# Two model blocks on one core: modulation sums on VectorE in the second block, grouped column sums, split spreads, and a last head-block in smaller chunks

## The chip, the cores and the metric

The kernel runs on one core of a Trainium2 chip. The metric is the device time of one execution in microseconds; lower is better. The program has no loop on the device: it is unrolled into 17908 instructions on the engines TensorE (PE, with its weight loads PEld), VectorE (DVE), ScalarE (ACT), GpSimd (POOL) and SyncE (SP, whose queue issues the weight loads).

## What is computed

For 256 tokens of width 1024, a first block of two layers (attention, recurrence and convolution, mixed and projected) is followed by a second block with a modulated norm, two mixers and an expert step. What the change touches belongs to the second block:

```python
def second_block(x, c, ctx, c_ctx, w_ada, b_ada, ...):
    s_c, s_cc = jax.nn.silu(c), jax.nn.silu(c_ctx)
    mod_lat = (s_c @ w_ada[l] + b_ada[l])[:, None, :]        # six parts of 1024: 0 to 5
    mod_ctx = s_cc @ w_ada[l] + b_ada[l]
    sh1, sc1, gt1, sh2, sc2, gt2 = jnp.split(mod_lat, 6, axis=-1)
    h_lat = rmsnorm(x, g_norm1) * (1.0 + sc1) + sh1          # parts 1 and 0, also for ctx
    ...                                                      # MLA attention and mLSTM on h_lat, h_ctx
    x = x + gt1 * (concat([mla_lat, ml_lat]) @ w_out)        # part 2
    h2 = rmsnorm(x, g_norm2) * (1.0 + sc2) + sh2             # parts 4 and 3
    return x + gt2 * peer(h2, w_pq, sub_keys, u, v)          # part 5

q = rmsnorm(q, g_qn); k = rmsnorm(k, g_kn)                   # per head over 128 + 64 values, in the MLA
```

In `peer` each token takes 16 experts for each of 8 heads; an expert is a row of 1024 values of `u` and 1024 of `v`. The row is gathered, its dot product with h2 goes through Gelu and a gate, and the result weighs the row of `v`.

## The kernel before

Activations are held transposed, 128 features on the partitions and 256 tokens in the free dimension, as 8 such tiles. Most projections are exact to fp32 by a split: ScalarE rounds a raw weight tile `w` (128x1024, 512 KB) into `wh` (L323), VectorE takes the rest `wl` (L268), and TensorE runs three fp32r matmuls for each pair (`wsplit`, `mm3`). Raw tiles come through `wload` (L314) on SP's queue into a ring of `NRAW` = 5 buffers with the tag `w`; the split pair has three buffers.

The order on each engine is made when the kernel is built. `at(us)` gives the following instructions a priority in planned time, `wload` puts a load 25 us ahead of its user, and a planner issues what is ready in that order, with its own model of durations and waits. On the chip each engine runs its list in order, so an instruction that waits holds everything behind it on that engine.

The six modulation parts are products of one vector with 1024x1024 matrices `wada`, eight tiles of 512 KB each:

- Parts 1, 0, 2, 4 and 3 run on TensorE in `part` (L963): eight loads through a ring of two buffers with the tag `wm`, 32 matmuls with 32 columns of weights, grouped four by four beside each other in the array, a copy (L966), two transposes. They are called by `hook`: the first three within layer 0, the last two within layer 1, at the planned times `mt`. With `np` = 5 the generator `modparts` has nothing to do.
- Part 5, the gate of the experts' result, runs during the expert step: `gate_sums` loads its tiles into the ring `w` and sums them on VectorE with `modsum` into `gs`, row by row times the scalar `sc0`, as a side task between the experts' dot products.

In the second block (`second`) the order of the program is: norms, `kvr`, `keys`, queries, `values` for both token sets (`proj` and `natural` use the ring `w`), the scans of the mLSTM gates, then the MLA heads. There `wkv` and two `wuq` tiles are loaded into the ring too and are used without a split until the heads and the value product `vml` are done. The sum of squares of each head's keys and queries is built with one-column matmuls, `ssk` and `ssq`, the squares as weights and a column of ones as the moving operand. The reciprocal roots go back to rows by spreads: 16 times VectorE scales the identity (`dg`, two buffers) and TensorE multiplies it by ones. Then come `mla` (scores, softmax, product) and `cells` (mLSTM, with a broadcast of the running maximum `Mr` by an fp32 matmul of 8 rows, 512 columns), interleaved by the string `PATTERN`, and `project` with weights `wo2`.

In `peer`, `experts` issues for each of 256 pairs of head-block and pick one gather on POOL (L1559) of 128 rows of 8 KB into one of nine buffers `G`, a dot product on VectorE (L1562), and after a chunk of picks the Gelu (L1566), the product with the gate, and for each pick a diagonal (L1575) and two fp32 matmuls of 512 columns. Chunks have four picks; in the last of 16 head-blocks they are 4, 4, 4, 2, 1, 1.

Of the kernel before, what the change touches and what calls it, by code (L numbers as in the profile page):

```python
# [8 lines left out]
F32 = mybir.dt.float32  # L9
F32R = mybir.dt.float32r  # L10
# [9 lines left out]
T = 256  # L20
# [105 lines left out]
def pack(inp):  # L126
# [97 lines left out]
    o["bgate"] = f["b_ada_2"][:, 5120:]  # L224
# [8 lines left out]
P = dict(np=5, glu=14, kv=35, kk=40, q=41, cmp=46, cmpd=5, w1n=62, cv0=32, cvd=35, att=57, attd=5, mix=137, woa=131, ln=145, pw2=160, wob=138, mod=5, ll=25000, sl=6000, nm=3, mt=(62, 80, 170, 243, 270), sp=29, L0=10, L1=196, S=369, B=500, cx=125, h1=2, h2=6, X=16, lri=37, lnk=7, tp=2, tq=0, ta=0, ml=40, mld=2.6, rt=36, g0=-32, ga=104, gb=161, gc=157)  # L233
# [7 lines left out]
def program(tc, A, dbg=lambda *a: None, stop=99):  # L241
# [66 lines left out]
    NRAW, NSP, NWA, NWM = 5, 3, 2, 2  # L308
# [175 lines left out]
    SLOTS = dict(g1=2048, g2=2048, g3=2048, g4=2048, g5=2048, g6=2048, gz4=1024, cz=1024, lu=2180, cs=512, silc=258,  # L484
# [459 lines left out]
    def modulation():  # L944
# [13 lines left out]
        def part(m):  # L958
# [18 lines left out]
            if m == 4:  # L977
                mg["pr"] = mk(cp, [128, 8], tag="mgpr")
                stt(mg["pr"], modt[:, 32:40, 0], 1.0, P2("g2"), add, mul)

        return [prep] + [lambda m=m: part(m) for m in (1, 0, 2, 4, 3)[:int(P["np"])]]

    def modsum(acc, m, k):

        w = wload(A["wada"][m, k], [128, 4, 256]).rearrange("p j c -> p (j c)")
        s = sc0[:, k:k + 1]
        if k == 0 and m != 5:
            ts(acc, w, s, None, mul)
        else:
            stt(acc, w, s, acc, mul, add)  # L990

    def modparts():
        for m in (4, 3)[int(P["np"]) - 3:]:
            acc = mk(b1, [128, 1024], tag="wm", bufs=NWM)
            for k in range(8):
                modsum(acc, m, k)
                if k == 7:
                    tp = psum("c", [128, 8])
                    for d in range(8):
                        mm(tp[:, d:d + 1], acc[:, d * 128:d * 128 + 128], ones[:, 0:1], True, True)  # L1000
                    o = modt[:, m * 8:m * 8 + 8, 0]
                    tt(o, tp, P2("bada")[:, m * 8:m * 8 + 8], add)
                    if m == 4:
                        mg["pr"] = mk(cp, [128, 8], tag="mgpr")
                        stt(mg["pr"], o, 1.0, P2("g2"), add, mul)
                if k % 2:
                    yield

    def second(C0, S):
# [187 lines left out]
        for d in range(2):  # L1197
            for b in range(2):
                tr(mnp[:, d, b], Mr[d][:, 256 + b * 128:384 + b * 128], ident[0:8, 0:8])
        emn = mk(b1, [128, 2, 2, 4], tag="emn")  # L1200
# [14 lines left out]
        values(0, X + 11)  # L1215
        keys(1, X + 15)

# [7 lines left out]
        ssk = psum("t", [128, 4, 4])  # L1225
        ckf = ckv.rearrange("p w t -> p (w t)")
        skf = skr.rearrange("p w t -> p (w t)")
        for h in range(4):
            acc = psum("acc", [128, 512])
            mm(acc, wkv[:, h * 128:(h + 1) * 128], ckf, True, True)  # L1230
            sq = slot(("blk", "cw2")[h % 2], 512)
            act.activation(sq, acc, AF.Square)
# [17 lines left out]
        ssq = psum("o", [128, 2, 4])  # L1250
        for h in range(0, 4, 2):
# [7 lines left out]
            for q in range(2):  # L1259
                for b in range(2):  # L1260
                    bs = slice(b * 128, b * 128 + 128)
                    mm(ssq[:, b, h + q:h + q + 1], sq[:, q, bs], ones[:, 0:1], True, False)
                    mm(ssq[:, b, h + q:h + q + 1], sqr[:, h // 2, bs], C(f"sel{q}"), False, True)
        values(1, X + 20)
        for q in range(4):
# [11 lines left out]

        v = mk(b1, [128, 24], tag="ssv")
        ts(v[:, 0:16], ssk.rearrange("p h q -> p (h q)"), 1.0 / 192, EPS, mul, add)
        ts(v[:, 16:24], ssq.rearrange("p b h -> p (b h)"), 1.0 / 192, EPS, mul, add)  # L1280
# [5 lines left out]
        krf = krr.rearrange("p w t -> p (w t)")  # L1286
        for h in range(4):
# [5 lines left out]
            tt(kn[:, h], kn[:, h], bc, mul)  # L1293
            hs = (lo64, hi64)[h % 2]
# [375 lines left out]
```

## Time and profile before

| what | value |
|---|---|
| median of 3 runs | 1406.02 us (1400.61 to 1406.84) |
| profiled execution | 1406.54 us, span 1404.6 us |
| TensorE busy | 1214.2 us, 86% |
| VectorE busy | 995.6 us, 71% |
| ScalarE busy | 528.6 us, 38% |
| GpSimd busy | 291.9 us, 21% |
| granted TensorE clock, mean | 0.938 |
| DMA | 387.50 MB, 276 GB/s over the span |

The busy time counts from an instruction's start to its modelled end; matmuls overlap, so a busy TensorE need not be at its peak. The granted clock is given as a share of 2.4 GHz. "DMA share" is the mean busy share of the core's 16 DMA engines. In a row, `c<-wm,silc` is the tile that is written and those that are read; a bracket at the end of a row tells how long the engine idled before it and what ended that. The chain of waits is the sequence of work that ended last, followed back from the last instruction.

### The profile page before, as it was taken

The page shows a single profiled execution, that of the slowest core. Times are in us where ns is not written, and L with a number is a line of the kernel's source. Part 1 is how long each engine was busy: PE and PEld are TensorE (multiplying, and loading weights), DVE is VectorE, ACT ScalarE, POOL GpSimd, SP SyncE. Part 2 cuts the span into 40 slices and gives each one's busy share as a digit, 9 for nine tenths or more (in the row PEclk, how much of TensorE's full clock was granted, in tenths as well). Part 3 has the DMA queues.
Part 4 walks back from the last instruction along what each step waited for, and adds up shares of the span by engine and source line. Part 5 has one row for each costly group of instructions (what it writes and reads, how often), then busy time and mean ns, then how long its engine had stood idle before and what let it go on. Part 6 is the DMA issues. An engine that isn't in the chain of part 4 may idle for free.

```text
span 1404.6 us, 17908 instructions
## 1 busy us (share of the span) xinstructions
PE 1214.2 (86%) x6050; PEld 798.9 (57%) x6050; DVE 995.6 (71%) x2454; ACT 528.6 (38%) x1130; POOL 291.9 (21%) x279
## 2 busy tenths in 40 slices
PE   6999899899979999999898978688868786877787
PEld 5987669698848888856795433243323332323333
DVE  6898865599987674455768766777676767667554
ACT  5635544344754544345453222222222222112211
POOL 0000000000000000000022444334444443443442
PEclk9999999899999987999999998999898999899989
DMA  8677446557403532410459999998999999999996
GB/s 323 193 282 263 168 162 218 169 170 245 133 21 108 165 98 75 132 33 1 151 193 423 421 422 421 421 407 349 421 422 412 422 421 413 414 422 421 417 409 273
DMA packets 71339, 387.50 MB, mean 276 GB/s; under 512 B 8401, under 2 KB 9425, under 8 KB 38226
## 3 DMA queue, kind: packets, MB, share of 16 engines
q0 software_dynamic: 36864, 268.45, 46.4%
q1 hardware_dynamic: 34386, 117.93, 24.8%
q8 instruction: 48, 0.79, 0.2%
q14 instruction: 41, 0.34, 0.1%
HBM read 385.30 MB, written 1.05 MB: 275 GB/s over the span
## 4 chain that ended last, share of the span: by engine, by line
PE 49%; DMA 27%; DVE 8%; issue 8%; POOL 5%; ACT 2%; POOLq 0%; DVEq 0%; SPq 0%; ACTq 0%
DMA G<-uv,eix 24%; PE acc L256 22%; PE acx L256 11%; PE s L256 6%; POOL G L1559 5%; DVE G L1562 4%; PE t L256 3%; PE o L256 2%; DMA wm<-wada 2%; PE c L963 2%; PE s L412 1%; DMA w<-wpq 1%; PE t L259 1%; PE c L256 1%; PE o L645 1%
## 5 line engine op out<-in xcount | busy, mean ns | idle before, releaser
L1562 DVE SCALAR_TENSOR_TENSOR G<-G,hn 128x1024 f32<-128x1024 f32 x256 | 313.5, 1225 | 176.9 <-DMA G<-uv,eix 173.5
L1559 POOL DMA_INDIRECT G<-uv,eix x256 | 284.4, 1111 | 443.0 <-PE o L256 134.4
L323 ACT ACTIVATE wh<-w 128x1024 fp32r<-128x1024 f32 (+2 forms) x142 | 148.5, 1048 | 192.2 <-PE acc L256 120.3
L268 DVE TENSOR_TENSOR wl<-w,wh 128x1024 fp32r<-128x1024 f32 (+2 forms) x142 | 171.5, 1210 | 62.6 <-ACT wh L323 61.3
L256 PE MATMUL t<-G,dg 128*128 128x512 f32 x256 | 146.7, 657 | 69.6 <-ACT dg L1575 69.6
L256 PE MATMUL c<-G,dg 128*128 128x512 f32 x256 | 147.2, 659 | 61.7 <-ACT dg L1575 61.7
L256 PE MATMUL acc<-hh,wh 128*128 128x256 f32 x608 | 178.5, 297 | 11.4 <-ACT wh L323 4.3
L256 PE MATMUL acc<-hh,wl 128*128 128x256 f32 x608 | 178.0, 295 | 2.0 <-DVE wl L268 2.0
L256 PE MATMUL acc<-hl,wh 128*128 128x256 f32 x608 | 166.5, 287 | 1.6 <-DVE hl L268 1.6
L1575 ACT ACTIVATE dg<-cst,w 128x128 f32<-128x128 f32 x256 | 89.4, 394 | 144.9 <-PE o L256 61.6
L256 PE MATMUL o<-G,dg 128*128 128x512 f32 x256 | 141.9, 638 | 0.0
L256 PE MATMUL acx<-G,dg 128*128 128x512 f32 x256 | 141.5, 636 | 0.0
L1566 ACT ACTIVATE s<-s 128x4 f32<-128x4 f32 (+1 forms) x66 | 13.5, 205 | 331.8 <-DVE G L1562 331.7
L256 PEld LDWEIGHTS t<-G,dg 128*128 128x128 f32 x256 | 50.2, 207 | 147.8 <-ACT dg L1575 95.3
L256 PEld LDWEIGHTS acc<-hh,wh 128*128 128x128 f32 x608 | 120.0, 198 | 19.5 <-ACT wh L323 5.1
L256 PEld LDWEIGHTS c<-G,dg 128*128 128x128 f32 x256 | 50.3, 207 | 133.7 <-ACT dg L1575 82.6
L256 PEld LDWEIGHTS acc<-hh,wl 128*128 128x128 f32 x608 | 120.4, 198 | 7.1 <-issue 2.8
L256 PEld LDWEIGHTS acc<-hl,wh 128*128 128x128 f32 x608 | 113.9, 193 | 5.3 <-issue 2.4
L262 DVE SCALAR_TENSOR_TENSOR g<-lu,pb,g 128x256 f32<-128x256 f32 x264 | 115.2, 480 | 0.2
L256 PEld LDWEIGHTS o<-G,dg 128*128 128x128 f32 x256 | 53.0, 207 | 69.5 <-issue 69.5
L256 PEld LDWEIGHTS acx<-G,dg 128*128 128x128 f32 x256 | 52.9, 206 | 68.9 <-issue 68.9
L1054 POOL MEMSET lu<- 128x16 f32 x1 | 0.4, 444 | 401.0 <-DVE g L262 401.0
(494 smaller groups left out, 2000.1 us busy)
## 6 DMA issues: line engine op xcount, KB each, us to landing
w<-w SPq DMA_DIRECT2D x64, 512.0 KB, 4.5
wm<-wada SPq DMA_DIRECT2D x40, 512.0 KB, 5.1
wa<-cw SPq DMA_DIRECT2D x16, 512.0 KB, 5.0
w<-woa SPq DMA_DIRECT2D x16, 512.0 KB, 3.5
w<-wpq SPq DMA_DIRECT2D x16, 512.0 KB, 3.5
w<-w2t SPq DMA_DIRECT2D x12, 512.0 KB, 3.5
w<-wob SPq DMA_DIRECT2D x8, 512.0 KB, 6.2
w<-w2v SPq DMA_DIRECT2D x8, 512.0 KB, 3.9
```

The lines of the kernel that those rows point to most:

```text
L256: pe.matmul(out, lhsT, rhs, start=start, stop=stop)
L259: pe.transpose(out, in_, ident)
L262: (e or dve).scalar_tensor_tensor(out, a, s, b, op0=op0, op1=op1)
L268: return (e or dve).tensor_tensor(out, a, b, op=op)
L323: act.activation(hi, w, AF.Copy)
L412: pe.matmul(acc[j:j + 32], ones[:, 0:32], sq[:, q] if square else srcs[i + q], start=i + q < 4, stop=i + q >= n - 4, tile_position=(0, j))
L645: pe.matmul(hps[32 * j:32 * j + 32], blk[:, q4 * 4 + j], w[:, j], start=q4 == 0, stop=q4 == 3, tile_position=(0, 32 * j))
L963: pe.matmul(acc[32 * j:32 * j + 32], sc[:, k], w[:, j], start=k == 0, stop=k == 7, tile_position=(0, 32 * j))
L1559: pool.indirect_dma_start(out=G, out_offset=None, in_=A["uv"], in_offset=bass.IndirectOffsetOnAxis(ap=eix[b][:, h, k:k + 1], axis=0))
L1562: dot = dve.scalar_tensor_tensor(G[:, 0:D], G[:, 0:D], 1.0, hn[b], op0=mul, op1=mul, accum_out=s[:, j:j + 1])
L1566: act.activation(s[:, 0:n], s[:, 0:n], AF.Gelu)
L1575: act.activation(dg, ident, AF.Copy, scale=w[:, j:j + 1])
```

## The change

Parts 2, 4 and 3 no longer run in the layers, and part 5 no longer in the expert step: `sums` computes all four on VectorE in the second block, in the order 4, 3, 2, 5. Each call of `more` loads one tile into the ring `w` and adds it; the calls stand after the projections, in the loops over heads, and after each step of `PATTERN`. Each part ends with four grouped matmuls, a copy and two transposes. The ring of raw tiles has four buffers instead of five, and the accumulator `ms` takes the room. The sums of squares of keys and queries become matmuls with 32 columns of ones, four heads beside each other in the array; their result goes back to columns by a matmul with `bd4`. The spread of the keys' roots is done with transposes, a split into two fp32r parts, and a broadcast from four rows; the broadcast of `Mr` in `cells` is split in the same way. Part 5 is turned into rows by `gate_rows` in the expert step. The last head-block has the chunks 4, 4, 2, 2, 1, 1, 1, 1.

```diff
-    NRAW, NSP, NWA, NWM = 5, 3, 2, 2
+    NRAW, NSP, NWA, NWM = 4, 3, 2, 2
...
-        return [prep] + [lambda m=m: part(m) for m in (1, 0, 2, 4, 3)[:int(P["np"])]]
...
+        return [prep] + [lambda m=m: part(m) for m in (1, 0)]
+
+    def sums(m):
+
+        acc = slot("ms", 1024)
+        for k in range(8):
+            w = wload(A["wada"][m, k], [128, 4, 256]).rearrange("p j c -> p (j c)")
+            if k == 0:
+                ts(acc, w, sc0[:, k:k + 1], None, mul)
+            else:
+                stt(acc, w, sc0[:, k:k + 1], acc, mul, add)
+            yield
+        tot = psum("c", [128, 256])
+        for j in range(4):
+            pe.matmul(tot[32 * j:32 * j + 32], ones[:, 0:32], acc[:, j * 256:j * 256 + 256], start=True, stop=True,
+                      tile_position=(0, 32 * j))
+        rows = mk(b1, [128, T], tag="tmp", bufs=3)
+        act.activation(rows, tot, AF.Copy)
+        tp = psum("c", [128, 2, 128])
+        for q in range(2):
+            tr(tp[:, q], rows[:, q * 128:q * 128 + 128], ident)
...
+        rest = [sums(m) for m in (4, 3, 2, 5)]
+
+        def more():
+
+            while rest and next(rest[0], 0) == 0:
+                rest.pop(0)
...
         kvr(0, S + 5)
+        more()
         keys(0, S + 9)
+        more()
...
+        id8 = slot("sc", 8, F32R)[0:8]
+        act.activation(id8, ident[0:8, 0:8], AF.Copy)
...
+            act.activation(Mh[d], Mr[d][:, 256:512], AF.Copy)
+            tt(Ml[d], Mr[d][:, 256:512], Mh[d].bitcast(F32), sub)
...
         for h in range(4):
+            more()
             acc = psum("acc", [128, 512])
             mm(acc, wkv[:, h * 128:(h + 1) * 128], ckf, True, True)
...
-            for q in range(4):
-                qs = slice(q * 128, q * 128 + 128)
-                mm(ssk[:, h, q:q + 1], sq[:, qs], ones[:, 0:1], True, False)
-                mm(ssk[:, h, q:q + 1], skf[0:64, qs], ones[0:64, 0:1], False, True)
+        mm(sumk, ones[0:64], skf[0:64], True, False)
+        for h in range(4):
+            pe.matmul(sumk[32 * h:32 * h + 32], ones[:, 0:32], sqk[:, h], start=False, stop=True, tile_position=(0, 32 * h))
...
+        for q in range(4):
+            mm(ss[:, q * 4:q * 4 + 4], rowk[:, q * 128:q * 128 + 128], C("bd4"), True, True)
...
         for h in range(4):
             bc = psum("s", [128, 512])
-            for q in range(4):
-                dg = mk(b1, [128, 128], tag="dg", bufs=2)
-                ts(dg, ident, rk[:, h * 4 + q:h * 4 + q + 1], None, mul)
-                mm(bc[:, q * 128:(q + 1) * 128], ones, dg, True, True)
+            one = id8[0:4, h:h + 1].broadcast_to([4, 128])
+            mm(bc, one, rkh, True, False)
+            mm(bc, one, rkl, False, True)
             tt(kn[:, h], kn[:, h], bc, mul)
+            more()
...
-                        mm(mb, ident[0:8, dh:dh + 1].broadcast_to([8, 128]), ml_[:, :, None, :].broadcast_to([8, 2, 2, 128]),
-                           True, False)
+                        for i, m in enumerate((Mh[d], Ml[d])):
+                            m = m.rearrange("p (t c) -> p t c", c=128)[:, :, None, :].broadcast_to([8, 2, 2, 128])
+                            mm(mb, id8[:, dh:dh + 1].broadcast_to([8, 128]), m, i == 0, False)
...
         for c in PATTERN:
             at(X + P["ml"] + P["mld"] * n)
             n += 1
             next(steps[c], None)
+            more()
...
-        def gate_sums():
-            for k in range(8):
-                modsum(gs, 5, k)
-                yield 1
+        def gate_rows():
             for hf in range(2):
                 gp = pst("g", [128, 512])
-                mm(gp, ones, gs[:, hf * 512:hf * 512 + 512], True, True)
+                for k in range(4):
+                    dg = mk(pp, [128, 128], tag="dg", bufs=3)
+                    ts(dg, ident, modt[:, 40 + hf * 4 + k, 0:1], None, mul)
+                    mm(gp[:, k * 128:k * 128 + 128], ones, dg, True, True)
+                    yield 1
...
-            experts(r % 8, r // 8, U0 + 16 * PICK * r, 4 if r == 0 else 2, (4, 4, 4, 4) if r < 15 else (4, 4, 4, 2, 1, 1))
+            experts(r % 8, r // 8, U0 + 16 * PICK * r, 4 if r == 0 else 2, (4, 4, 4, 4) if r < 15 else (4, 4, 2, 2, 1, 1, 1, 1))
```

## Rows read from the trace of the kernel before

**Rows 1.** Stages: PE, PEld, DVE, ACT, POOL busy us, PEclk, DMA share, GB/s

```profile
419.00:541.00 122.00, 115.13 (x789) 100.49 (x788) 87.86 (x218) 62.06 (x112) 3.03 (x8) 0.93 0.40 125
541.00:573.00 32.00, 31.80 (x142) 27.99 (x142) 8.06 (x20) 10.26 (x21) 0.00 (x0) 0.73 0.17 55
573.00:613.00 40.00, 37.44 (x145) 25.70 (x144) 23.82 (x51) 16.11 (x23) 0.00 (x0) 0.96 0.37 119
613.00:665.00 52.00, 51.09 (x237) 33.27 (x236) 28.77 (x102) 29.39 (x83) 0.96 (x1) 0.90 0.00 1
724.00:1391.00 667.00, 531.37 (x1322) 241.48 (x1321) 461.09 (x1149) 162.65 (x403) 284.05 (x256) 0.93 1.00 414
```

**Rows 2.** Parts: chain 155 to 270 (shares; start, us), waits on `wm`, VectorE's timeline

```profile
by line: PE acc L256 32.0%; DMA wm<-wada 20.0%; PE acx L256 13.7%; PE c L963 9.2%; PE s L256 5.7%; PE t L259 3.0%; PE o L811 2.0%; DVE g L749 2.0%; PE s L412 1.9%; DVE g L262 1.2%; issue 1.2%; ACT L745 1.1%; DVE wl L268 1.0%; DVE g L268 0.9
...
183.68 1.00 PE c L963 x16
...
  DMA wm<-wada: 23.8, 20
...
255.91 3.22 DVE L460 SCALAR_TENSOR_TENSOR g<-XT,pb,t 128x256 f32<-128x256 f32 x8 [4.24 <-PE t L256]
```

**Rows 3.** Timeline: convolution's sums copied, its projection begins; layer 0, then 1

```profile
182.56 0.38 ACT L415 ACTIVATE tmp<-s 128x256 f32<-128x256 f32 x1
201.96 0.60 PE L256 MATMUL acc<-g,wa 128*128 128x256 f32 x2
...
412.55 0.39 ACT L415 ACTIVATE tmp<-s 128x256 f32<-128x256 f32 x1
427.31 2.08 PE L256 MATMUL acx<-g,wa 128*128 128x256 f32 x4
```

**Rows 4.** Chain, heads (start, us, what, records); last row by stage

```profile
542.62 2.29 PE t L256 x16
545.96 3.30 PE t L256 x16
549.26 2.86 PE acx L256 x6
552.12 7.92 PE t L256 x32
561.19 4.77 PE acc L256 x16
569.11 3.47 PE o L256 x32
...
550.00:560.00 10.00, 10.00 (x38) 9.32 (x37) 0.00 (x0) 0.00 (x0) 0.00 (x0) 0.50 0.00 0
```

**Rows 5.** Chain: fp32r of 512 columns, broadcast with mask, fp32 of 512 columns

```profile
588.62 4.08 PE acx L256 x18
613.82 1.26 PE s L256 x3
624.51 1.72 PE s L256 x4
```

**Rows 6.** One line's operations: ns min/median/max, first and last start

```profile
L262 DVE SCALAR_TENSOR_TENSOR gs<-w,sc,gs x8: 1265/1280/1285, 895.8 to 954.0; 128x1024 f32<-128x1024 f32 x8
```

**Rows 7.** SP's queue in order of time; landing of `wada` tiles

```profile
508.76 0.33 SPq L314 DMA_DIRECT2D w<-wukv  x1
527.90 10.94 SPq L314 DMA_DIRECT2D w<-w2v  x4
...
DMA to landing us min/median/max: 3.2/5.2/9.6
```

**Rows 8.** Expert step: `wada` loads (ns, first and last), a dip, the end

```profile
L314 SPq DMA_DIRECT2D w<-wada x8: 328/328/328, 725.4 to 900.8; - x8
...
950.00:960.00 10.00, 7.16 (x17) 3.27 (x16) 7.37 (x20) 3.48 (x7) 2.61 (x3) 0.83 0.64 220
...
1385.58 1.13 PE L256 MATMUL t<-G,dg 128*128 128x512 f32 x2 [1.12 <-ACT dg L1575]
```

More of the change, by code (lines that the diff above doesn't have):

```diff
@@ L992, in modparts @@
-    def modparts():
-        for m in (4, 3)[int(P["np"]) - 3:]:
-            acc = mk(b1, [128, 1024], tag="wm", bufs=NWM)
-            for k in range(8):
[L996 to L1007, printed above, removed]
+        return [prep] + [lambda m=m: part(m) for m in (1, 0)]
@@ L1199, in second @@
                 tr(mnp[:, d, b], Mr[d][:, 256 + b * 128:384 + b * 128], ident[0:8, 0:8])
+        id8 = slot("sc", 8, F32R)[0:8]
+        act.activation(id8, ident[0:8, 0:8], AF.Copy)
+        Mh = [slot(n, T, F32R)[0:8] for n in ("rows", "ang")]
+        Ml = [slot(n, T, F32R)[0:8] for n in ("silc", "hidr")]
+        for d in range(2):
+            act.activation(Mh[d], Mr[d][:, 256:512], AF.Copy)
+            tt(Ml[d], Mr[d][:, 256:512], Mh[d].bitcast(F32), sub)
         emn = mk(b1, [128, 2, 2, 4], tag="emn")
@@ L1215, in second @@
         values(0, X + 11)
+        more()
         keys(1, X + 15)
+        more()
         accq = proj(1, (3, 4), X + 10)
@@ L1249, in second @@
             rope2(u[:, r], qr[:, r])
-        ssq = psum("o", [128, 2, 4])
+        sumq = psum("o", [128, T])
+        sqs = []
         for h in range(0, 4, 2):
@@ L1258, in second @@
             act.activation(qn[:, h:h + 2], acc, AF.Copy, scale=P2("gqn"))
[L1259 to L1263, printed above, removed]
+            sqs += [sq[:, 0], sq[:, 1]]
+        for h in range(4):
+            pe.matmul(sumq[32 * h:32 * h + 32], C(f"sel{h % 2}").broadcast_to([128, 32]), sqr[:, h // 2], start=True, stop=False,
+                      tile_position=(0, 32 * h))
+        for h in range(4):
+            pe.matmul(sumq[32 * h:32 * h + 32], ones[:, 0:32], sqs[h], start=False, stop=True, tile_position=(0, 32 * h))
+        rowq = slot("cw2", T)
+        act.activation(rowq, sumq, AF.Copy)
+        more()
         values(1, X + 20)
+        more()
         for q in range(4):
@@ L1276, in second @@
             so.append(th)
+        ss = psum("s", [128, 24])
+        for q in range(4):
+            mm(ss[:, q * 4:q * 4 + 4], rowk[:, q * 128:q * 128 + 128], C("bd4"), True, True)
+        for b in range(2):
+            mm(ss[:, 16 + b * 4:20 + b * 4], rowq[:, b * 128:b * 128 + 128], C("bd4"), True, True)
         v = mk(b1, [128, 24], tag="ssv")
-        ts(v[:, 0:16], ssk.rearrange("p h q -> p (h q)"), 1.0 / 192, EPS, mul, add)
-        ts(v[:, 16:24], ssq.rearrange("p b h -> p (b h)"), 1.0 / 192, EPS, mul, add)
+        ts(v, ss, 1.0 / (32 * 192), EPS, mul, add)
         rk = rsqrt(b1, v, [128, 24], "rk", 1)
@@ L1286, in second @@
         krf = krr.rearrange("p w t -> p (w t)")
+        rp = psum("s", [4, 512])
+        for q in range(4):
+            tr(rp[:, q * 128:q * 128 + 128], rk[:, q * 4:q * 4 + 4], ident)
+        rkh, rkl = slot("blk", 512, F32R)[0:4], slot("cw2", 512, F32R)[0:4]
+        act.activation(rkh, rp, AF.Copy)
+        tt(rkl, rp, rkh.bitcast(F32), sub)
         for h in range(4):
             bc = psum("s", [128, 512])
-            for q in range(4):
-                dg = mk(b1, [128, 128], tag="dg", bufs=2)
-                ts(dg, ident, rk[:, h * 4 + q:h * 4 + q + 1], None, mul)
-                mm(bc[:, q * 128:(q + 1) * 128], ones, dg, True, True)
+            one = id8[0:4, h:h + 1].broadcast_to([4, 128])
+            mm(bc, one, rkh, True, False)
+            mm(bc, one, rkl, False, True)
             tt(kn[:, h], kn[:, h], bc, mul)
+            more()
             hs = (lo64, hi64)[h % 2]
@@ L1420, in project @@
                 yield
-        steps = dict(m=mla(), c=cells(), a=project(0), x=modparts())
+        steps = dict(m=mla(), c=cells(), a=project(0))
         n = 0
@@ L1427, in second @@
             next(steps[c], None)
-        for c in "mcxa":
+            more()
+        while rest:
+            more()
+        for c in "mca":
             for _ in steps[c]:
@@ L1593, in peer @@
         gtb = mk(pp, [128, 2, 512], tag="gtb")
-        gs = mk(pp, [128, D], tag="gs")
-        at(B + 10)
-        pool.memset(gs, 0.0)
-        nc.sync.dma_start(gs[0:1], A["bgate"])
-        def gate_sums():
-            for k in range(8):
-                modsum(gs, 5, k)
-                yield 1
+        def gate_rows():
             for hf in range(2):
                 gp = pst("g", [128, 512])
-                mm(gp, ones, gs[:, hf * 512:hf * 512 + 512], True, True)
+                for k in range(4):
[3 more added lines that the diff above has]
+                    yield 1
                 act.activation(gtb[:, hf], gp, AF.Copy)
@@ L1621, in peer @@
             if r == 3:
-                side.append(gate_sums())
+                side.append(gate_rows())
             if r == 10:
@@ L1645, in hook @@
             return
-        for i in range(min(int(P["nm"]), len(steps)) if l == 0 else len(steps)):
-            at(P["mt"][int(P["np"]) - len(steps)])
+        for i in range(len(steps)):
+            at(P["mt"][2 - len(steps)])
             steps.pop(0)()
```

30 lines of the change are left out of this document (13 added, 17 removed).

## The prediction, written before the changed kernel had run

> **What bounds the kernel now.** I read the busy time of the engines by stage first, then the chain that ended last, then single waits. The stages [rows 1] show two kinds of kernel. From 724 to 1391 us the DMA share is 1.00 at 414 GB/s: the expert gathers run and the transfer sets the pace, while TensorE is busy 531 of 667 us and VectorE 461. Before that TensorE sets it: in the second block, 419 to 665 us, it is busy 115.1 of 122, 31.8 of 32, 37.4 of 40 and 51.1 of 52 us, while VectorE has 34, 24, 16 and 23 us idle, 97 together. The third thing to see is where TensorE is busy with little: from 550 to 560 it is busy 10.00 us at a granted clock of 0.50, the lower of its two levels, with VectorE and ScalarE at 0.00 [rows 4].
>
> The sum is made against the profiled execution's own 1406.54 us (span 1404.6 and 1.94 around it), 0.5 above the median of the three runs.
>
> **1. Three modulation parts leave the layers.** Before, parts 2, 4 and 3 run on TensorE in layer 0's attention and at the start of layer 1. Of the chain from 155 to 270 us, waits on their weights are 20.0% and their matmuls 9.2%, 33.6 of 115 us [rows 2]: the upper bound. What comes back is less, since something else is late next. In layer 1 VectorE has the norm's diagonals ready, but the spread's matmuls stand behind a part that waits for its load, and VectorE waits 4.24 us for them until 255.91 [rows 2]. Without that the four matmuls need some 1.2 us, start included: 2.9 to 3.0 saved, and with the two later bursts of the part, at 1.00 us each [rows 2], 4.9. In layer 0 I compare the same stretch in both layers, from the copy of the convolution's sums to its projection: 182.56 to 201.96 = 19.4 us with parts between, 412.55 to 427.31 = 14.8 without [rows 3]. Attention runs beside it on VectorE and ScalarE and doesn't get faster, so I take 4 of the 4.6. Layer term: **-9**, from -3 to -16.
>
> **2. Column-grouped sums.** Removed are 32 one-column matmuls for the keys, 2.29 + 3.30 + 7.92 = 13.5 us in the chain, and 16 for the queries, 3.47 [rows 4]: 17.0 on TensorE, all on the path, since VectorE idles beside them. Added: one full 512-column sum of the rope part at 0.86 us (1.72 for four records of that form [rows 5]); four grouped ones of 512 and eight of 256, by the grouped form's 16 records of 256 columns in 1.00 us [rows 2] about 1.0 each; six small ones on `bd4`, 12 records at 0.11 (3.47/32), 1.3. Together 4.2, net -12.8. The projections between them ran at the lower clock too: 22 records of 256 columns took 2.86 + 4.77 = 7.6 us [rows 4] where half of a 512-column record, 0.215, each would be 4.7, so 2.9 more if the clock now stays up: -15.7. ScalarE is next in line, and is busy 10.3 us in the whole stretch [rows 1], shorter than TensorE's new 15 or so. I take **-16**; if the clock stays down -10, at best -19.
>
> The Trainium skill, in TensorE: Matmul & The Clock Gate (Part 1), says that the clock follows the engine's activity and falls in idle gaps. Read by it, removing filler could also cool the array. The row of the stretch says that busy one-column work didn't keep it up, so by the row nothing is lost; by the rule a gap behind late weights costs, and that is the third rival below.
>
> **3. Split spreads.** The keys' spread loses 16 diagonals and 16 small fp32 matmuls for two copies, four transposes and eight fp32r matmuls of 512 columns at 0.23 (4.08/18 [rows 5]): the matmul time is equal within 1 us, but the stop and go on the two diagonal buffers goes; it is most of the 2.6 us that TensorE idles between 573 and 613 [rows 1]. In the cells, eight fp32 broadcasts, 1.26 each with the mask [rows 5], become two fp32r ones, 0.46 with 0.12 for the mask: 0.68 each, 5.4 in all. The scalars `id8`, `Mh`, `Ml` cost five short operations beside TensorE work. Neither form at K=4 or 8 in fp32r stands in the trace; bounds are 0.23 (the 128-row form) and 0.43 (a pass of fp32). At the upper bound the cells gain 2.3. Of the 8 together a third is hidden by VectorE and ScalarE, so **-5**, from 0 to -8.
>
> **4. What is added in the second block.** 32 sums of 128x1024 on VectorE, at 1.28 us [rows 6] 41 us, against 97 idle, and 32 loads of 512 KB through the ring of raw weights, which goes from five buffers to four. Their cover is VectorE's idle time, and it is uneven. Loads of this ring are issued in the order of the program. After `wkv` (508.76 [rows 7]) and the two `wuq`, which stay in their buffers until the heads are done, one buffer is left. Five sum tiles pass through it ahead of the values' weights: 5 x (5.2 landing [rows 7] + 1.3) = 32 us from about 516, so the values' weights, issued from 527.9 before [rows 7], go at about 549 and are split near 557, when TensorE, 16 us earlier now, would want them: 5 lost. Later 16 sums fall, by the pattern, beside the cells: 28.8 + 20.5 = 49.3 of 52 us of VectorE there. Behind each stand softmax maxima, reciprocals and scales, and TensorE waits for those; a third of the 16 lands on the path, 7. The four short ends (grouped sums, copy, two transposes) cost 1 together. A load that comes late stops VectorE as it stopped TensorE in the parts, 23.8 us in 20 waits [rows 2]. Bounds: 0 (all hidden) and 32 x (1.28 + 1.19) = 79. I take **+13**, nearer to the lower end, because VectorE's idle total is more than twice the sums. In the layers the fourth buffer costs nothing: a tile is used every 2.9 us, so four reach 11.5 us ahead and landing takes 5.2; its cover is that lead, and 1 us would go where a split waits.
>
> **5. The gathers.** Eight loads of part 5, 4.19 MB, leave the stage [rows 8]; at 421 GB/s they are 10.0 us of a queue that is never idle. The first came at 725, as the queue was filling, so 9. From 950 to 960 the share was 0.64 at 220 GB/s [rows 8]: TensorE stood behind a late score weight whose load had queued behind these eight on SP, and gathered rows weren't freed. That is 201 of 421 for 10 us, 4.8, and the dip's edges on both sides some 2.6 more; I take 6. The new `gate_rows` (eight diagonals, eight small matmuls, two copies) lies beside the transfers. **-15**, from -8 to -18.
>
> **6. The last head-block.** Before the last chunk of four, TensorE waits 1.12 us for its weights [rows 8] and is then busy to the end. Chunks of two start it earlier; two more Gelu calls and products at 0.2 us lie in the gaps. **-1.5**, from 0 to -2.
>
> **Sum.** -9 - 16 - 5 + 13 - 15 - 1.5 = -33.5: **1373 us**.
>
> **Rivals.** (a) *All sums hidden*: VectorE's idle time takes them and the loads arrive in time; step 4 costs 1 or 2, and with 3 more from the layers the time is 1373 - 12 - 3 = 1358. For it: 97 us idle. Against: the crowded cells. (b) *Starved second block*: the one free buffer holds the sums, then the values' and the output gate's weights back, TensorE waits and its clock falls to the lower level, at which the grouped sums and heads take twice as long: step 2 falls to -10, step 4 rises to +27, 1373 + 20 = 1393. For it: the weights' order [rows 7] and the clock of 0.50 [rows 4]. Against: TensorE has the values' product with `wkv` to do meanwhile. This is the case to which the skill's clock rule would lead. (c) *The sums become the path*, the slower end: every sum and a wait of 1.19 before it stops VectorE in a stretch where TensorE waits for it, 79 us in place of 13: 1373 + 66 = 1439. It decides from step 4 above 46.5, half of all sums and waits; the idle 97 us speak against it. (d) *The gathers don't get shorter*, because the issue on GpSimd or TensorE paces them: step 5 is 0, 1388. Against: a share of 1.00 over 667 us.
>
> **Chances.** Forecast (1364 to 1384) 0.45; (a) 0.20; (b) and (d) together 0.22; gains lost to within the bound 0.08; (c) 0.05. About 0.5%, 7 us, is what a measurement here can tell from no change. Slower by more than that 0.05, within 0.08, faster 0.87. The range leaves out less than 2 in 10: from 1352, all of (a) but its best, to 1394, the end of (b).
>
> **What would show it.** Step 1: no `wada` load under 260 us but those of parts 1 and 0, layer 1's first projection some 9 us earlier. Step 2: the heads' stretch, 31 us from first head to last query sum, takes about 15 at a clock near 1.0. Step 3: no diagonals in the key spread. Step 4: busy VectorE in the cells near 50 of their time and, if it costs, waits of VectorE on `w<-wada` and a longer cells stretch. Step 5: no `wada` load among the gathers, no dip, from first gather to last 15 us less. Wrong would be: second block not shorter than before, or the DMA share under 1 in the gathers.

## The result, and the profile after

The changed kernel takes 1385.77 us (median of 4 runs, 1383.0 to 1386.17) beside 1403.33 for the kernel before (4 runs, 1400.61 to 1406.84). The ratio is 0.9867, with a 95% interval of 0.9845 to 0.9889, so it is 18.7 us faster (15.6 to 21.8): the forecast side and inside the range of 1352 to 1394, but only 56% of the 33.5 us that the sum had. The profiled execution shortens from a span of 1404.6 to 1383.6 us.

The page of the changed kernel: TensorE has 24 us less to do than before, VectorE 24 more.

```profile
span 1383.6 us, 17499 instructions
PE 1190.4 (86%) x5826; PEld 778.7 (56%) x5826; DVE 1019.2 (74%) x2475; ACT 530.0 (38%) x1139; POOL 300.1 (22%) x278
```

Its stages, the lines that answer to [rows 1] (stretch, its length, then PE, PEld, DVE, ACT and POOL busy, granted clock, DMA share, GB/s): the heads from the first head's matmul to the last query sum, the values up to the last matmul that turns the sums of squares back into columns (`bd4`), the spreads up to the matmul behind the first softmax, the cells up to the output projection, and the gathers from the first issue to the last.

```profile
531.92:550.90 18.98, 18.11 (x82) 8.87 (x80) 10.88 (x20) 12.47 (x27) 1.80 (x1) 1.00 0.44 156
550.90:568.80 17.90, 17.00 (x71) 12.70 (x70) 11.34 (x17) 9.89 (x14) 0.00 (x0) 0.90 0.68 220
568.80:600.57 31.77, 27.03 (x100) 15.03 (x99) 27.81 (x46) 8.07 (x16) 0.00 (x0) 0.89 0.72 245
600.57:651.96 51.39, 47.86 (x248) 33.17 (x249) 39.16 (x112) 32.44 (x87) 0.00 (x0) 0.97 0.36 123
710.70:1361.30 650.60, 525.80 (x1322) 239.43 (x1321) 448.50 (x1140) 160.57 (x399) 292.15 (x256) 0.92 1.00 413
```

The heads run at full clock now, where [rows 4] had 0.50. The next thing to see is the third line: VectorE is busy for 27.8 of 31.8 us there and TensorE has 4.7 us idle. The chain of that stretch (568.8 to 601 us, shares by engine and line) says why:

```profile
by line: DVE ms L261 34.4%; DMA w<-wada 30.1%; DVE g L267 14.2%; issue 6.8%; PE acx L255 3.0%; DVE onat L261 2.8%; ACT blk L1348 2.7%; PE s L255 2.5%; DVE mmx L1343 2.4%; DVE cw L267 1.1%; DVE mmx L261 0.5%; DVE modt L267 0.5%; DVEq L261 0.
```

The sums and the loads that they wait for are two thirds of it. The waits on loads of the ring in the second block that come to 2 us or more (what waited, for what, us, times, longest); those of VectorE are for the sums' tiles alone:

```profile
DVE ms L261 <- DMA w<-wada: 14.6, 10, 2.9
ACT wh L322 <- DMA w<-w2o: 4.6, 2, 2.8
DVE ms L264 <- DMA w<-wada: 2.3, 2, 1.6
```

To see where each kernel wins and loses, I divide the profiled executions at five marks: the load of the context tokens (the end of layer 1's attention), the first head's matmul, the first softmax maximum on VectorE, the first gather, and the last dot product of a gathered row. Times in us, with the ratio to the kernel before from all runs; the kernels below the second line are the experiments.

| kernel | to the context load | to the first head | to the first maximum | to the first gather | to the last dot | to the end | ratio (95%) |
|---|---|---|---|---|---|---|---|
| before | 419.4 | 120.0 | 68.4 | 115.9 | 669.6 | 11.3 | 1 |
| changed | 413.1 | 118.8 | 66.3 | 112.5 | 663.5 | 9.4 | 0.9867 (0.9845 to 0.9889) |
| e1_heads | 419.3 | 116.9 | 54.2 | 106.8 | 669.0 | 12.8 | 0.9867 (0.9843 to 0.9891) |
| e2_move | 410.7 | 118.4 | 71.0 | 119.8 | 660.5 | 11.4 | 0.9992 (0.9980 to 1.0005) |
| e3_p5g | 411.3 | 118.5 | 66.6 | 115.1 | 674.3 | 9.2 | 0.9970 (0.9951 to 0.9988) |
| e4_lay | 423.3 | 121.8 | 56.5 | 111.1 | 661.9 | 9.9 | 0.9849 (0.9825 to 0.9872) |
| e4_lay5 | 419.5 | 119.3 | 59.5 | 107.8 | 663.4 | 9.3 | 0.9787 (0.9759 to 0.9816) |
| e5_noload | 411.5 | 117.4 | 63.0 | 108.9 | 661.3 | 9.3 | 0.9769 (0.9742 to 0.9797) |
| e6_none | 413.9 | 117.7 | 55.9 | 106.6 | 662.4 | 9.4 | 0.9731 (0.9704 to 0.9758) |
| e9_early | 418.7 | 117.1 | 60.1 | 110.9 | 659.9 | 9.3 | 0.9794 (0.9772 to 0.9816) |
| e10_both | 419.2 | 117.2 | 60.1 | 110.9 | 661.5 | 9.9 | 0.9778 (0.9759 to 0.9796) |
| e11_spread | 412.2 | 118.5 | 64.9 | 111.3 | 657.4 | 9.3 | 0.9808 (0.9784 to 0.9831) |

Prices below are taken from the ratios (0.001 is 1.4 us); a difference of two ratios is uncertain by some 3 to 5 us. The stages come from one execution each and say where a difference lies: the executions of one kernel spread over 2 to 13 us. The filler kernel e7_fill has one run and no ratio, so it isn't in the table.

### The profile page after: what moved, and what is told of

Its sections match the earlier page's. It is cut to its first block, busy times and chain, and to the rows that moved or that the text cites. A ratio compares the mean times of both kernels' runs of the same rounds, so it can differ in the third digit from the quotient of the medians.

```text
span 1383.6 us, 17499 instructions
## 1 busy us (share of the span) xinstructions
PE 1190.4 (86%) x5826; PEld 778.7 (56%) x5826; DVE 1019.2 (74%) x2475; ACT 530.0 (38%) x1139; POOL 300.1 (22%) x278
## 4 chain that ended last, share of the span: by engine, by line
PE 46%; DMA 28%; issue 9%; DVE 9%; POOL 5%; ACT 3%; POOLq 0%; DVEq 0%; SPq 0%; ACTq 0%
DMA G<-uv,eix 26%; PE acc L255 22%; PE acx L255 9%; POOL G L1597 5%; PE s L255 5%; DVE G L1600 3%; PE t L255 1%; PE o L255 1%; DMA w<-wada 1%; PE s L411 1%; PE t L258 1%; PE c L255 1%; DVE ms L261 1%; PE c L962 1%; PE o L810 1%
## 5 line engine op out<-in xcount | busy, mean ns | idle before, releaser
L1597 POOL DMA_INDIRECT G<-uv,eix x256 | 293.7, 1147 | 521.8 <-PE acc L255 163.4
L1604 ACT ACTIVATE s<-s 128x4 f32<-128x4 f32 (+2 forms) x68 | 13.9, 205 | 337.2 <-DVE G L1600 337.1
L255 PEld LDWEIGHTS acc<-hh,wh 128*128 128x128 f32 x608 | 121.5, 200 | 11.3 <-ACT hh L461 3.8
```

What stands on the lines that cost most here:

```text
L255: pe.matmul(out, lhsT, rhs, start=start, stop=stop)
L1597: pool.indirect_dma_start(out=G, out_offset=None, in_=A["uv"], in_offset=bass.IndirectOffsetOnAxis(ap=eix[b][:, h, k:k + 1], axis=0))
L1604: act.activation(s[:, 0:n], s[:, 0:n], AF.Gelu)
```

## The experiments

**One part at a time.** Edits are against the changed kernel; `...` marks lines that are left out.

e1_heads keeps only the grouped sums and the split spreads; parts 2, 4 and 3 are back in `part`, part 5 in the expert step, with the old chunks:

```diff
-    NRAW, NSP, NWA, NWM = 4, 3, 2, 2
+    NRAW, NSP, NWA, NWM = 5, 3, 2, 2
...
-        return [prep] + [lambda m=m: part(m) for m in (1, 0)]
...
+        return [prep] + [lambda m=m: part(m) for m in (1, 0, 2, 4, 3)]
...
-        rest = [sums(m) for m in (4, 3, 2, 5)]
+        rest = []
...
```

> Only the grouped sums and the split spreads (steps 2 and 3 of the prediction); all modulation parts, the ring of five and the last chunks stay as before. By the sizes of the prediction -16 - 5 = -21 us against the kernel before. By the trace of the changed kernel, whose stretch from first head to last query sum shrank from 33 to 19 us while the cells' stretch shrank by 3, about -17. A rival: VectorE or a late weight is next in line there, and less than -10 arrives at the end. The heads' stretch itself should take 17 to 18 us, with the granted clock at 1.00 in it, and the stages outside 530 to 665 us should not move.

Measured: 0.9867, -18.7 us, as much as the whole change. The heads take 21.6 us at a granted clock of 1.00, not the 17 to 18 expected: the weights of the values are early here, and TensorE runs products with them from 552.0 to 553.1 and from 554.0 to 557.5 us, between the last sums of the queries. The time from the first head to the first maximum falls by 14.2, the rest of the second block by 9.1 after it and 3.1 ahead of it. The stages outside are those of before within 1.5 us. The stages add up to 26 us and not 18.7; the profiled execution was the fastest of the six, 3.5 us under their median. So steps 2 and 3 together were sized about right (-21), and everything else in the change sums to nothing, within the 3 to 5 us that two ratios can tell.

e2_move does the rest without them: `ssk`, `ssq`, the diagonals and the fp32 broadcasts are back, with the old chunks.

```diff
-        sqk = slot("g5", 2048).rearrange("p (h t) -> p h t", h=4)
-        sumk = psum("t", [128, 512])
+        ssk = psum("t", [128, 4, 4])
...
-                            mm(mb, id8[:, dh:dh + 1].broadcast_to([8, 128]), m, i == 0, False)
+                        mm(mb, ident[0:8, dh:dh + 1].broadcast_to([8, 128]), ml_[:, :, None, :].broadcast_to([8, 2, 2, 128]),
+                           True, False)
```

> Only the move of the four parts (steps 1, 4 and 5): sums on VectorE in the second block and the ring of four, with the one-column sums, the diagonal spreads, the fp32 broadcasts and the last chunks as before. By the sizes of the prediction -9 + 13 - 15 = -11 us against the kernel before. By the trace of the changed kernel the layers give 6, the sums cost about 12 and the gathers give 6 to 9: about 0 to -3. If the sums hide better beside the longer one-column matmuls, in which VectorE stood idle for 12 us, it is -6 or better.

Measured: 0.9992, -1.1 us (-2.8 to +0.7), where the sum of the prediction had -11. Its profiled execution was 9 us faster than the median of its runs, so its stages flatter it; which stage the other runs lose is open. The two kernels agree: with either form of the heads, the move of the parts is worth nothing that can be told.

e3_p5g puts part 5 back among the gathers:

```diff
...
-        rest = [sums(m) for m in (4, 3, 2, 5)]
+        rest = [sums(m) for m in (4, 3, 2)]
...
+            for k in range(8):
+                w = wload(A["wada"][5, k], [128, 4, 256]).rearrange("p j c -> p (j c)")
+                stt(gs, w, sc0[:, k:k + 1], gs, mul, add)
+                yield 1
...
```

> The changed kernel with part 5 back among the gathers (24 sums in the second block in place of 32). By the sizes of the prediction it gives up 15 us of the gathers and saves a quarter of 13: +12 against the changed kernel. If the gathers' gain is only the 4.19 MB (10 us) and stalls of the same size come elsewhere, as the trace of the changed kernel suggests (6 us less from first gather to last dot product), +3 to +7. The eight loads should be seen among the gathers again, and the rate there tells whether the stalls go with them.

Measured: 0.9970, 14.5 us slower than the changed kernel: near the prediction's +12, and at least twice the +3 to +7 that I had read from the trace. The stretch of the gathers is the longest of all, 674.3 us against 669.0 to 669.6 in the two kernels that have these loads and five raw buffers. Four tiles of part 5 fill the ring of four from 729 us on, and the next score weights go only at 882.9; with five buffers (the kernel before) two of them went from 741.6 to 763.6. So this run is not a clean price of step 5. In its profiled execution, part 5 among the gathers and the ring of four together make that stretch longer than either alone.

e4_lay puts parts 2, 4 and 3 back on TensorE in the layers, and e4_lay5 gives it the fifth raw buffer again. e4_lay:

```diff
...
-        return [prep] + [lambda m=m: part(m) for m in (1, 0)]
...
+        return [prep] + [lambda m=m: part(m) for m in (1, 0, 2, 4, 3)]
...
-        rest = [sums(m) for m in (4, 3, 2, 5)]
+        rest = [sums(5)]
...
```

e4_lay5 besides:

```diff
-    NRAW, NSP, NWA, NWM = 4, 3, 2, 2
+    NRAW, NSP, NWA, NWM = 5, 3, 2, 2
...
-        acc = slot("ms", 1024)
+        acc = slot("wm", 1024, bufs=NWM)
```

> The changed kernel with parts 2, 4 and 3 back on TensorE in the layers; only part 5's eight sums stay in the second block, the ring has four buffers. By the sizes of the prediction it gives up 9 and saves three quarters of 13: -1, no difference. By the trace of the changed kernel, where the layers gave 6 and the stretch between heads and cells cost 12, it gives up 6 and saves 9: about -3. If most of the 12 belongs to the first sums, which hold up the values' weights in the ring, it is slower by up to 4.

> As the run with parts 2, 4 and 3 back in the layers, but with five raw buffers, the accumulator of part 5 lying in the ring of the parts' own weights. If four buffers cost nothing in the layers, as the prediction has it, no difference to that run (1384). In that run's trace the layers end 4 us later than in the kernel before; if that is the ring, and the ring also holds up the second block, -4 to -10: 1374 to 1380, the fastest of all so far.

Measured: 0.9849 and 0.9787, that is -21.2 and -29.9 us against the kernel before. e4_lay agrees with the smaller sizes (2.5 us faster than the changed kernel, within what can be told). The fifth buffer is worth 8.7 us, uncertain by some 5, and part of it lies where the prediction had put nothing: in the layers. The stages 125 to 150 and 200 to 215 us, first with four buffers, then with five:

```profile
125.00:150.00 25.00, 20.78 (x185) 17.43 (x182) 22.06 (x42) 10.34 (x23) 0.00 (x0) 0.97 0.75 257
200.00:215.00 15.00, 11.63 (x94) 8.68 (x94) 9.16 (x37) 5.89 (x13) 0.00 (x0) 0.89 0.20 69
```

```profile
125.00:150.00 25.00, 25.00 (x195) 20.74 (x195) 21.59 (x55) 15.15 (x36) 0.00 (x0) 1.00 0.59 202
200.00:215.00 15.00, 14.86 (x101) 13.24 (x95) 7.61 (x16) 5.61 (x9) 0.00 (x0) 1.00 0.23 73
```

TensorE loses 4.2 and 3.2 us there with four. In the changed kernel, whose layers carry no loads of parts 2, 4 and 3, TensorE is busy for 25.00 of 25 and 15.00 of 15 us in these stretches, so by these three executions the price needs both, four buffers and the parts' loads on the same queue.

**What the sums cost.** e6_none has the four parts as their bias alone:

```diff
-        rest = [sums(m) for m in (4, 3, 2, 5)]
+        rest = []
+        for m in (4, 3, 2, 5):
+            act.activation(modt[:, m * 8:m * 8 + 8, 0], P2("bada")[:, m * 8:m * 8 + 8], AF.Copy)
...
```

e5_noload keeps every sum but reads a resident tile in place of each load:

```diff
-            w = wload(A["wada"][m, k], [128, 4, 256]).rearrange("p j c -> p (j c)")
+            w = XT.rearrange("p k t -> p (k t)")[:, 0:1024]
```

> The changed kernel with the four parts' products left out altogether (no loads, no sums, no grouped matmuls; those parts are set to their bias alone), so that step 4 costs nothing. By the prediction's size of step 4 it is 13 us under the changed kernel. By the runs before, in which the stretch from the second block's start to the first gather took 278 us with steps 2 and 3 alone and 298 in the changed kernel, it is 20 under. If the sums were well hidden, 2 or less.

> The changed kernel with all 32 sums on VectorE, but each reads a tile that is already in the array's memory (part of the token tile) in place of one of the 32 loads: the sums' values mean nothing, their time stays, and the ring of four carries weights alone. If the cost of step 4 is VectorE's time, it is within 4 us of the changed kernel. If it is the ring, in which 32 tiles pass in the order of the program ahead of the values' and the output's weights, it gains most of the 20 and comes within 4 of the kernel without sums. The prediction gave 5 of 13 to the ring and 7 to VectorE.

Measured: 0.9731 and 0.9769. Step 4 costs 0.0136, 19.1 us. The loads are 13.8 of it and VectorE's time with the four short ends 5.3. The stages say it less sharply: from the context load to the first gather it is 297.6 us in the changed kernel, 289.3 without the loads and 280.2 without the sums, 8.3 and 9.1; what the runs have beyond that lies in the layers and the gathers, where no sum runs, or in the choice of the execution. So both cost: the loads 8 to 14 us, the engine with the ends 5 to 9. e5_noload takes away the buffers that they hold and the transfers together; for the ring speaks that the DMA share was 0.72 at 245 GB/s in the crowded stretch (third line of the stages), where the gathers reach 1.00 at 413. SP's queue in order of time shows how the ring delays (start, us from the first issue to the last, tile, count): the changed kernel first, then the same weights without sums.

```profile
510.48 0.33 SPq L313 DMA_DIRECT2D w<-wukv  x1
512.76 3.53 SPq L313 DMA_DIRECT2D w<-wuq  x2
525.12 18.84 SPq L313 DMA_DIRECT2D w<-wada  x5
546.98 6.43 SPq L313 DMA_DIRECT2D w<-w2v  x4
555.10 0.33 SPq L313 DMA_DIRECT2D w<-wada  x1
556.90 7.25 SPq L313 DMA_DIRECT2D w<-w2o  x4
567.22 38.70 SPq L313 DMA_DIRECT2D w<-wada  x20
```

```profile
521.65 20.27 SPq L313 DMA_DIRECT2D w<-w2v  x4
546.00 11.74 SPq L313 DMA_DIRECT2D w<-w2o  x4
```

Five sum tiles pass one after the other and the values' weights go at 547.0, 25 us later than without them; the output's weights are 11 later; then twenty sum tiles follow at one in 2 us, and VectorE stops for them with the spreads' products in its list behind. VectorE in 568.80 to 600.57, with sums that need no load and then without sums, is busy 29.9 and 20.1 us:

```profile
568.80:600.57 31.77, 26.54 (x98) 13.60 (x96) 29.94 (x45) 12.99 (x24) 0.00 (x0) 0.89 0.20 66
```

```profile
568.80:600.57 31.77, 29.27 (x110) 17.53 (x109) 20.13 (x38) 17.41 (x36) 0.00 (x0) 0.95 0.20 67
```

It is the same stretch of time, not of work: their first softmax maxima come at 591.9 and 587.5 us, for 598.2 in the changed kernel. From the first head to that maximum it is 66.3 us in the changed kernel, 63.0 without the loads and 55.9 without the sums, so by these three executions the sums themselves cost twice what their loads do in this stretch.

**The clock in layer 0.** The layers of the changed kernel end 6 us earlier, not 9, and in the profiled execution the lost part is layer 0's. TensorE from 195 to 205 us, in the kernel before and then in the changed one:

```profile
195.00:200.00 5.00, 3.37 (x40) 1.51 (x37) 3.97 (x18) 1.96 (x5) 0.00 (x0) 1.00 0.77 247
200.00:205.00 5.00, 4.87 (x36) 4.26 (x33) 3.48 (x10) 2.87 (x6) 0.00 (x0) 1.00 0.49 172
```

```profile
195.00:200.00 5.00, 2.49 (x11) 1.83 (x11) 4.39 (x13) 2.24 (x5) 0.00 (x0) 0.50 0.00 0
200.00:205.00 5.00, 5.00 (x23) 4.69 (x23) 1.99 (x3) 1.75 (x3) 0.00 (x0) 0.61 0.00 0
```

The parts' matmuls were filler in the attention's gaps. Without them the convolution's projection begins 1.6 us earlier (200.38 for 201.96 [rows 3]), but at the lower level, and at 214.4 us both kernels stand at the same matmul. e7_fill, whose one run took 1388.14 us, puts bursts that nobody reads in their place, each of four grouped matmuls with 32 columns of ones as weights:

```diff
+                    if l == 0 and b == 1 and bi == 2:
+                        filler(pTs.rearrange("p a t -> p (a t)"), 512)
...
+                if l == 0:
+                    fill[0](cv[:, i], 256)
```

> The changed kernel with eight short bursts of matmuls on TensorE near the end of layer 0's attention whose result nobody reads (four behind the last copies of the softmax weights, four behind the convolution's norm), in the place where part 2's matmuls were. If the engine's activity keeps the clock up, the granted clock between 185 and 215 us is near 1.0 (0.67 and 0.87 in the changed kernel, 1.00 before) and layer 1's first projection begins 1 to 2 us earlier than 253.6. If the clock there has nothing to do with these gaps, it stays low or the bursts only make it later, by up to 4 us.

Measured, the stretch up to 205 us:

```profile
195.00:200.00 5.00, 3.59 (x39) 1.46 (x37) 2.66 (x11) 1.72 (x4) 0.00 (x0) 1.00 0.00 0
200.00:205.00 5.00, 5.00 (x49) 3.59 (x42) 3.64 (x11) 2.74 (x6) 0.00 (x0) 1.00 0.01 3
```

The clock stays up. One execution could owe that to chance, since the clock here differs between executions of the same layers. But from 195 to 200 us it is 1.00 in all six kernels with the parts in the layers and in the one with the filler, and in the six without either it is 0.50 in four, 0.79 in e2_move and 0.84 in e3_p5g. So it goes with what the engine does there, though not by that alone. As an improvement the filler failed: the attention's result was copied at 202.33 in place of 200.62, and layer 1's first projection began at 254.54 where the changed kernel had 253.62. In e2_move and e3_p5g, which kept more of the clock with no filler, that projection began at 251.34 and 251.79.

**The dip that came back.** The gathers should have lost a dip of 220 GB/s [rows 8]. They did, and got another: 188 GB/s from 760 to 765 us, 50 us after the first gather. GpSimd stood idle before its next issue, and TensorE's last long row ahead of it is a score product (GpSimd's issue; TensorE's last score product, and its next product of gathered rows; the stretch):

```profile
762.54 0.94 POOL L1597 DMA_INDIRECT G<-uv,eix  x1 [7.20 <-DVE eix L261]
```

```profile
760.26 0.28 PE L255 MATMUL acc<-hh,wl 128*128 128x256 f32 x1
760.38 1.02 PE L255 MATMUL c<-G,dg 128*128 128x512 f32 x2
```

```profile
760.00:765.00 5.00, 5.00 (x16) 2.47 (x15) 3.04 (x10) 3.19 (x6) 1.68 (x2) 1.00 0.54 188
```

From 753.0 to 760.4 TensorE did score products and nothing of the gathered rows. In the kernel before, the last two heads' scores were copied at 780.9 and 947.8 us, since their weights queued behind `wada`; now all weights are there early and they are copied at 754.8 and 760.6. e11_spread holds the scores of the last four heads back, each behind the product of a gathered row in the head-block before (`marks`), and changes nothing else:

```diff
...
+                    marks.append(last.ins)
...
-            if r < 6:
+            if r < 2:
                 scores(r + 2, U0 + 16 * PICK * r - 12)
+            elif r < 6:
+                with tc.issue_after(marks[16 * r - 12]):
+                    scores(r + 2, U0 + 16 * PICK * r - 12)
```

> The changed kernel with one thing else: the score products of the expert step's fourth and later heads are held back on TensorE behind a product of gathered rows a head-block earlier, instead of running as soon as their weights are there. If the dip 50 us after the first gather (188 GB/s from 760 to 765 us in the changed kernel, GpSimd idle 7.2 us before its next gather) comes from a block of 7 us of score products that TensorE runs ahead of the gathered rows, the dip goes and 3 to 6 us with it: 1380 to 1383 against the changed kernel's 1386. If it comes from VectorE's routing, as the named releaser of that wait says, the dip stays and nothing is gained.

Measured: 0.9808, 8.3 us faster than the changed kernel, more than expected. The same place in the stage, and the whole stage:

```profile
757.00:762.00 5.00, 4.30 (x11) 1.67 (x10) 3.23 (x9) 1.59 (x5) 3.27 (x3) 1.00 1.01 419
706.92:1352.13 645.21, 517.37 (x1322) 236.62 (x1321) 448.01 (x1140) 160.49 (x399) 290.45 (x256) 0.93 1.01 416
```

No dip, 416 GB/s in place of 413 and 5.4 us less from first gather to last. It was TensorE's order; the releaser that the wait names (the experts' indices on VectorE) was not the one that mattered. The other traces agree: each of the seven other kernels with part 5 moved and the scores as they were has such a dip 40 to 60 us after the first gather (222 to 321 GB/s over 10 us), and neither of the two that hold the scores back has it there.

**Two attempts at a better kernel.** e9_early is e4_lay5 with part 5's sums asked for before the heads, e10_both adds the held scores. e9_early against e4_lay5:

```diff
         kvr(0, S + 5)
         more()
+        more()
         keys(0, S + 9)
+        more()
         more()
```

> The kernel with parts 2, 4 and 3 in the layers and five raw buffers (1375), with part 5's eight sums asked for earlier: two instead of one behind each of the first two projections, so that none is left for the heads. There the last two loads stood ahead of the values' weights, which were issued 7 us later than in the kernel with no sums (531.8 against 525.0), and the heads' stretch took 27.7 in place of 21.6 us. If that order is the price, -3 to -6: 1369 to 1372; if the sums cost the same wherever they are, no difference.

> Both together: part 5's sums early, parts 2, 4 and 3 in the layers, five raw buffers, and the score products held back. If the two are independent, the sum of their gains against 1375: -6 to -12, 1363 to 1369, and 2.5 to 3% under the kernel before. If the dips only move again, no faster than the earlier sums alone.

Measured: 0.9794 and 0.9778, both the same as e4_lay5 (0.9787) within what can be told. The values' weights go at 518.8 us in e10_both, earlier than the 525.0 of e1_heads, and the heads still end no sooner: from the first head to the first maximum it is 60.1 us against 54.2 with no sums. So the order of the last two loads was not the price; what the price is stays open. The held scores gave nothing here, where other dips remain (three stretches of 10 us at 329 to 365 GB/s between 130 and 190 us after the first gather). The fastest kernels that compute the whole result are these three, 2.1 to 2.2% under the kernel before and 0.7 to 0.9% under the changed one.

## Why the prediction was right in sign and half in size

The three prices that the runs separate: steps 2 and 3 gave -18.7 (predicted -21), step 4 cost +19.1 (+13), and steps 1, 5 and 6 together, which is e6_none against e1_heads, gave -19.1 (-25.5). Short of the forecast by 2.3, 6.1 and 6.4: 14.8 us, and by the stages two steps, 5 and 4, carry nearly all of it.

**Step 5 failed: about -7 where I had -15.** From the first gather to the last dot it is 663.5 us for 669.6 in the profiled pair, and 659.9 to 663.4 in the other kernels with part 5 moved and the scores as they were. About the 9 us for the bytes of eight loads came, by the issues: first gather to last 650.6 for 659.5. The 6 for the dip didn't. I read its cause rightly (a late score weight behind `wada` on SP), but not what follows when the weights are early: the score products bunch up at the start of the stage and make the same dip there. With them held back (e11_spread) it is 657.4, 12 us less than before. The prediction's own sign of error, "the DMA share under 1 in the gathers", is the row of 0.54.

**Step 4 was mis-sized: +19 where I had +13, and most of what was missing is the ring.** I gave 5 to the ring, 7 to VectorE and 1 to the short ends; the runs give 13.8 to the loads and 5.3 to the other two, the stages of the second block 8.3 and 9.1. The time of the values' weights was right to 2 us (547.0, forecast 549). The error was to count that delay once: the ring keeps the order, so the output's weights were late too, and the twenty tiles behind them stopped VectorE ahead of the spreads. The crowded cells, where I had put 7, did not come: VectorE is busy 39.2 of 51.4 us there, not 50, because 24 of the 32 sums were done before, and that stretch got shorter (56.7 us from the first maximum to the output projection before, 53.8 now). Rival (c), the sums as the path, is what happened between 569 and 598 us: sums and their waits are 64.5% of the chain there, some 21 us, far from its 79. The 46.5 from which it was to decide is where the whole sum comes to nothing (33.5 + 13), and not, as the prediction says, half of all sums and waits, which is 39.5.

**Step 1 came to -5 to -9 in the layers.** Six executions without the three parts reach the context load at 410.7 to 413.9 us, before 419.4. The start of layer 1 is as worked out, 4.85 us earlier for the 4.9 of [rows 2]; the first projection, before and changed:

```profile
258.47 0.58 PE L256 MATMUL acc<-hh,wh 128*128 128x256 f32 x1
253.62 0.58 PE L255 MATMUL acc<-hh,wh 128*128 128x256 f32 x1 [1.63 <-ACT hh L461]
```

The 4 us of layer 0, taken from the difference between the two layers [rows 3], were not there in the profiled execution: the stretch took 18.2 us, not 14.8. They go with the clock: the convolution's projection began at 198.24 and 198.66 in the two executions with 0.79 and 0.84, 3.7 and 3.3 us before the 201.96 of [rows 3], and at 199.65 to 200.93 in the four with 0.50. I had weighed the rule of the Trainium skill (TensorE: Matmul & The Clock Gate, Part 1), that the clock follows the engine's activity and falls in its gaps, for the heads alone. In the layers the traces agree with it: 1.00 from 195 to 200 us with the parts or the filler, 0.50 to 0.84 without.

**Steps 2 and 3 held, as a sum.** The heads' stretch, from the start of the first head's matmul to that of the last query sum, went from 32.8 us (539.4 to 572.2) to 18.4, at a granted clock of 1.00; forecast was 31 to 15. The stretch before, with its clock of 0.74:

```profile
539.41:572.50 33.09, 32.89 (x145) 28.15 (x143) 9.05 (x20) 11.42 (x22) 0.00 (x0) 0.74 0.21 64
```

Part of the 18.4 is the late values' weights, which leave TensorE nothing else to do between the sums; with early ones the stretch is 21.6 (e1_heads). No run takes the two steps apart. By the stages of e1_heads the gain after the first maximum, 9.1, was larger than the 5 of step 3; why stays open.

**Step 6 held.** From the last dot product to the end: 11.3 us before, 9.4 now, and 9.2 to 9.9 in every kernel with the new chunks against 11.3 to 12.8 with the old: -2 for the forecast -1.5.

Of the rivals, (a) fell; (d) comes nearest: the gathers got shorter by half of what was forecast. (b) had the ring's mechanism, but the stages from the heads to the cells have mean clocks of 0.89 and above, and step 2 kept its gain.

## What to carry to other kernels

Price work that is moved behind a shared ring of buffers by what it does to the order of loads, to the end of the stage: here 32 sums on an engine with idle time cost 5 us by the runs and 9 by the stages, and their loads, priced at 5, cost 14 or 8. When a late transfer that causes a stall is removed, ask what it was holding back; here it held score products apart that bunch up without it. And try the parts of a change alone: two of its parts were worth all of it, and keeping three of the moved parts in the layers, with the fifth buffer, gained 11 us more.

## What the runs showed of the hardware that was not expected

The same layers were granted different clocks in different executions: from 185 to 200 us the changed kernel shows 0.67 and e3_p5g, whose layers have the same code, 0.95, and layer 1 starts 1.8 us earlier in the latter.

The engine counts as busy in one-column matmuls at a clock of 0.50 [rows 4]; twelve grouped matmuls with 32 columns of ones (and one full one for the rope part) in the place of 48 such took the heads' stretch to 1.00, in e1_heads too, which changes nothing ahead of it. Only the clock column told that the busy engine did little.

e5_noload and e6_none spread over 2.4 and 1.7 us in six runs, every kernel with the loads of these parts somewhere over 6.6 us or more in five to 23 (the changed kernel: 3.2 in four). What in the loads makes the time scatter wasn't examined.
